# GDN chunk matrices kept in SBUF between preparation and merge, with smaller convolution and inversion buffers

## The chip, the cores and the metric

The kernel runs on one core of a Trainium2 chip. The metric is the device time of one execution in microseconds. Engines are named as in the profile: PE is TensorE, PEld its weight loads, DVE is VectorE, ACT is ScalarE, POOL is GpSimd, SP is SyncE, which here only issues DMAs.

## The reference, cut to what matters

One layer of a diffusion backbone: 256 context tokens and 1024 latent tokens of width 1024; norm and modulation, one input projection, two groups of four heads (a gated DeltaNet, "GDN", and a retention), output projection, SwiGLU, final norm. The change concerns the triangular solve inside the GDN:

```python
A = jnp.where(strict, jnp.einsum('nbhid,nbhjd->nbhij', kb, kc) * decay, 0.0)
rhs = jnp.concatenate([vc * bc[..., None], kb * jnp.exp(G)[..., None]], axis=-1)
sol = lax.linalg.triangular_solve(A + jnp.eye(CHUNK, dtype=A.dtype), rhs,
                                  left_side=True, lower=True, unit_diagonal=True)
...
def step(S, xs):
    u_c, w_c, q_c, qk_c, k_c, gl = xs
    v_new = u_c - jnp.einsum('bhck,bhkv->bhcv', w_c, S)
    o = jnp.einsum('bhck,bhkv->bhcv', q_c, S) + jnp.einsum('bhij,bhjv->bhiv', qk_c, v_new)
    S = gl * S + jnp.einsum('bhck,bhcv->bhkv', k_c, v_new)
    return S, o
```

It runs over the sequence in both directions. q, k and v come from the projection through a centred convolution of five taps and a Silu.

## The kernel before

The kernel works with chunks of 128 tokens: ten chunks (0 and 1 are context), four heads, two directions. For each chunk, head and direction it builds a 128 x 128 triangular matrix, inverts it, and stores the inverse in DRAM (`sd`) for the scan.

Order of the stages that matter. Convolutions: `conv_block` (L596) projects one head of 128 channels for all tokens on PE into the two PSUM banks `b2`, copies each piece twice with ACT (L608 to `u`, L609 to `y`), adds the other four taps on DVE (L615) and applies Silu on ACT (L618). It runs four times for k, four times for q (latent tokens only), four times for v. `y` comes from `newy` (L620), three buffers in the pool CV. A buffer comes free when its heads' transposes have read it: `kstat` (L625) for k, `qstat` (L681) for q, the vT transposes (L868) for v, and when the k or q store (L654, L697) is done. The order of the q loop is written out: the statistics of one head stand behind the convolution of the next and behind `ada_rest` (L487), a modulation product on DVE.

The gate projection rg (`token_major` for groups 6 and 7, L704 and L706) follows q, the z projection (groups 8 and 9, L891) follows the merges, four more projections (groups 2 to 5) follow two scan steps (L999 to L1002). Each projects tiles of 128 tokens with 24 matmuls of 256 columns, stored through `res` (two buffers in R1) to `rd` or `zd`.

The solve goes by three batches of chunks, `BATCH` (L714): sixteen, sixteen and eight matrices per direction.
- `pre(t)` (L719) loads k and q of a chunk, forms the products kk and kq on PE, and for each direction loads the decay row `gw` (L732), masks it on POOL into `e` (L736), takes the exponential on ACT (L740), multiplies kk by it on DVE into `ut` (L744) and kq into `sp` (L746). `ut` is stored to `un` in DRAM (L747), `sp` to `sd` (L749).
- `invert(b)` (L755) loads the diagonal 32 x 32 blocks of all matrices of the batch from `un` into `yr`, one block per partition (L763), copies them to `L`, sets `X` to the identity on POOL (L767, L768) and inverts by 31 pairs of DVE instructions (L777, L779). `X` and its transpose go to `xd` in DRAM (L783).
- `blocks(b)` (L785) loads all of `un` back to SBUF as `U` (L795), clears `t64` (L797), and loads the inverted blocks from `xd` into U and t64 (L799, L800).
- `merge(b)` (L804) builds the inverse of 64 and then of 128 from the blocks with small matmuls (L819 to L846), and stores U to `sd` (L850).

`solve(0)` and `solve(1)` stand ahead of the v convolutions; preparation of batch 2 (chunks 5 and 6) stands behind them and behind the closing of CV; then come `merge(0)`, `invert(2)`, `merge(1)`, `merge(2)`.

SBUF is handed out by pools that open and close from the left (`gu`, `gi`, `gp`, `g2`, weights) and from the right (`gs`, `cv`, `rope`, `gm`, later the scan's). A tile waits for the tiles that lay at its place. The program is written in dependent order, and the framework fixes each engine's order when the kernel is built, by a model of the times; on the chip every engine and every DMA queue runs its own order strictly. The SP queue carries the loads of `pre`, the `un`, `sp`, `xd` transfers and the scan's loads; the ACT queue carries the stores of q, k, v, `res` and merged U, and most weights.

Of the kernel before, what the change touches and what calls it, by code (L numbers as in the profile page):

```python
# [8 lines left out]
F32 = mybir.dt.float32  # L9
# [3 lines left out]
ALU = mybir.AluOpType  # L13
# [4 lines left out]
P = 128  # L18
# [4 lines left out]
NTOK = NCTX + NLAT  # L23
TT = NTOK // P
LT = NLAT // P
H = 4
# [12 lines left out]
def build(nc, tc, ap, dbg=None, stop=None, marks=None):  # L39
# [151 lines left out]
    try:  # L191
# [428 lines left out]
        def newy():  # L620
            return CV.tile([P, NTOK], F32, tag="y", name="y", bufs=3)

# [27 lines left out]
        for h in range(H):  # L650
            y = newy()
# [64 lines left out]

        un = [dr.tile([P, 2, len(ch) * H, P], F32, tag="un%d" % b, name="un%d" % b) for b, ch in enumerate(BATCH)]

        def pre(t):  # L719
            b, c = where[t]  # L720
            kc = load(GP, kd[t], "kc", 2)
            pk = bank_b("kk")
            for h in range(H):
                T.matmul(pk[:, h * P:(h + 1) * P], kc[:, h, :], kc[:, h, :], start=True, stop=True)
            if t >= 2:
                qc = load(GP, qd[t - 2], "qc", 2)
                pq = bank_b("kq")
                for h in range(H):
                    T.matmul(pq[:, h * P:(h + 1) * P], kc[:, h, :], qc[:, h, :], start=True, stop=True)
            for d in range(2):  # L730
                gw = GP.tile([P, H, P], F32, tag="gw", name="gw", bufs=2)
                SY.dma_start(gw.rearrange("p h i -> p (h i)"),  # L732
                             grow_d[c8(t, d), :].rearrange("a b -> (a b)").partition_broadcast(P))
                e = GP.tile([P, H, P], F32, tag="e", name="e", bufs=2)
                sg = 1 if d == 0 else -1
                G.affine_select(out=e, in_=gw, compare_op=ALU.is_ge, fill=FAR, base=0,  # L736
                                pattern=[[0, H], [sg, P]], channel_multiplier=-sg)
                for h in range(H):
                    col = t * 8 + d * 4 + h
                    S.activation(e[:, h, :], e[:, h, :], AF.Exp, bias=sm["nG"][:, col:col + 1])  # L740
                if t >= 2:
                    sp = GP.tile([P, H, P], F32, tag="sp", name="sp", bufs=2)
                ut = GU.tile([P, H, P], F32, tag="ut", name="ut", bufs=2)
                V.tensor_tensor(ut.rearrange("p h i -> p (h i)"), pk, e.rearrange("p h i -> p (h i)"), ALU.mult)  # L744
                if t >= 2:
                    V.tensor_tensor(sp.rearrange("p h i -> p (h i)"), pq, e.rearrange("p h i -> p (h i)"), ALU.mult)  # L746
                SY.dma_start(un[b][:, 1 - d, c * H:(c + 1) * H, :], ut)  # L747
                if t >= 2:
                    SY.dma_start(sd[t, :, 8 - 8 * d], sp.rearrange("p h i -> p (h i)"))  # L749
# [5 lines left out]
        def invert(b):  # L755
# [6 lines left out]
            for k in range(4):  # L762
                SY.dma_start(yr[k:2 * nb:4].rearrange("r (i j) -> r i j", j=32),  # L763
                             un[b][q32[k]].rearrange("i e u j -> (e u) i j")[:, :, q32[k]])
            L = GI.tile([P, 1024], F32, tag="L", name="L", bufs=3)
            X = GI.tile([P, 1024], F32, tag="X", name="X", bufs=2)
            G.memset(X, 0.0)  # L767
# [4 lines left out]
            for j in range(31):  # L772
                n = 31 - j
                tmp = GI.tile([P, 256], F32, tag="tmp%d" % b, name="tmp", bufs=2)
                t3 = tmp[:2 * nb, :n * (j + 1)].rearrange("p (i c) -> p i c", c=j + 1)
                sh = [2 * nb, n, j + 1]
                V.tensor_tensor(t3, bc(m(L)[:, j + 1:, j], sh, 2), bc(m(X)[:, j, :j + 1], sh, 1), ALU.mult)  # L777
                xs = m(X)[:, j + 1:, :j + 1]
                V.tensor_tensor(xs, xs, t3, ALU.subtract)  # L779
            XT = GI.tile([P, 1024], F32, tag="L", name="XT", bufs=3)  # L780
            V.tensor_copy(m(XT), X[:2 * nb].rearrange("p (i j) -> p j i", j=32))
# [3 lines left out]
        def blocks(b):  # L785
# [6 lines left out]

            at = G2 if b == 1 else GM
            uu = at.tile([P, 2, len(BATCH[b]), H, P], F32, tag="U", name="U%d" % b, bufs=1)
            SY.dma_start(uu.rearrange("p e c h j -> p e (c h) j"), un[b])  # L795
            tt = at.tile([P, 2, nu, 64], F32, tag="t64", name="t64", bufs=1)
# [7 lines left out]
        def merge(b):  # L804
# [11 lines left out]
            for n in range(nu):  # L816
                for d, p, a, bb in pairs:
                    ca = (a % 2) * 32
                    T.matmul(ps1[q[bb], n * 32:n * 32 + 32], u[d][q[a], n, q[bb]], t[d][q[a], n, ca:ca + 32],  # L819
                             start=True, stop=True)  # L820
            xt1 = GM.tile([P, 16, 32], F32, tag="xt1", name="xt1", bufs=1)
            V.tensor_scalar(xt1.rearrange("p n j -> p (n j)")[:, :nu * 32], ps1[:, :nu * 32], -1.0, None, ALU.mult)
# [14 lines left out]
            for n0 in range(0, nu, 8):  # L837
                ps1, ps2 = bank_b("m2"), bank_b("m2")
                xt2 = GM.tile([P, 8, 64], F32, tag="xt2", name="xt2", bufs=1)
                for n in range(8):  # L840
# [34 lines left out]
        rope = RP.tile([P, TT, P], F32, tag="rope", name="rope")  # L875
        GM = pool("gm", side="right")
        for t in BATCH[2]:
            pre(t)
# [794 lines left out]
```

## Time and profile before

| What | us |
| --- | --- |
| runs | 1485.98, 1486.84, 1479.36 |
| median of the runs | 1485.98 |
| profiled execution | 1482.3 |
| its span | 1480.4 |
| PE busy | 1399.8 |
| DVE busy | 981.1 |
| ACT busy | 610.5 |
| POOL busy | 579.5 |

The span runs from the first to the last instruction of the profiled execution; the execution's own time also holds what lies around it, 1.9 us. In the span the first k convolution's results are copied at 129 us, the last q convolution's at 262 us; preparation's first multiplication stands at 278.9 us, the last v transposes at 372.6 us, the first merge's matmuls begin at 403.7 us, the last merge's end at 475 us. Lines in the order of time give start, duration, engine, line, operation, output and inputs, the number of merged instructions, and in brackets the idle time before them with what ended it.

### The profile page before, as it was taken

The page shows a single profiled execution, that of the slowest core. Times are in us where ns is not written, and L with a number is a line of the kernel's source. Part 1 is how long each engine was busy: PE and PEld are TensorE (multiplying, and loading weights), DVE is VectorE, ACT ScalarE, POOL GpSimd, SP SyncE. Part 2 cuts the span into 40 slices and gives each one's busy share as a digit, 9 for nine tenths or more (in the row PEclk, how much of TensorE's full clock was granted, in tenths as well). Part 3 has the DMA queues.
Part 4 walks back from the last instruction along what each step waited for, and adds up shares of the span by engine and source line. Part 5 has one row for each costly group of instructions (what it writes and reads, how often), then busy time and mean ns, then how long its engine had stood idle before and what let it go on. Part 6 is the DMA issues. An engine that isn't in the chain of part 4 may idle for free.

```text
span 1480.4 us, 24179 instructions
## 1 busy us (share of the span) xinstructions
PE 1399.8 (95%) x8919; PEld 1200.6 (81%) x8919; DVE 981.1 (66%) x1909; ACT 610.5 (41%) x1336; POOL 579.5 (39%) x493
## 2 busy tenths in 40 slices
PE   7999999997889999998799899999999999999997
PEld 2798888876879999898588688877888888788886
DVE  6568797379772535789677886746555554657586
ACT  5543554765222111446444533323333333454454
POOL 0130010220102353254135588999555553335321
PEclk9999999999899999999799999999999999999999
DMA  9537686696878625985633265765232242786863
GB/s 338 186 104 230 178 245 204 199 297 191 256 193 272 247 69 185 411 328 181 217 115 115 85 215 210 266 240 178 107 107 107 107 150 74 239 279 195 306 202 114
DMA packets 170710, 293.95 MB, mean 199 GB/s; under 512 B 43528, under 2 KB 93912, under 8 KB 166496
## 3 DMA queue, kind: packets, MB, share of 16 engines
q1 hardware_dynamic: 119040, 248.98, 49.3%
q10 hardware_dynamic: 49072, 35.83, 7.7%
q0 software_dynamic: 2480, 7.60, 1.4%
q8 instruction: 70, 1.15, 0.3%
q14 instruction: 48, 0.39, 0.1%
HBM read 206.60 MB, written 85.77 MB: 197 GB/s over the span
## 4 chain that ended last, share of the span: by engine, by line
PE 40%; POOL 6%; DMA 2%; issue 1%; DVE 1%; ACT 0%; POOLq 0%; DVEq 0%; ACTq 0%
PE ffn L1362 7%; PE ffn L1360 6%; PE ffn L1361 6%; PE fo L1486 5%; PE fo L1488 5%; PE fo L1487 5%; DMA wd<-tw 2%; PE op L1219 2%; PE op L1220 2%; PE op L1221 2%; POOL ws L1333 1%; POOL tw L1414 1%; POOL tw L1413 1%; POOL tw L1416 1%; POOL tw L1415 1%
## 5 line engine op out<-in xcount | busy, mean ns | idle before, releaser
L371 PE MATMUL tm<-whi,hhi 128*128 128x256 f32 (+1 forms) x704 | 200.8, 290 | 7.2 <-ACT res L532 3.6
L372 PE MATMUL tm<-wlo,hhi 128*128 128x256 f32 (+1 forms) x704 | 200.4, 287 | 1.3 <-DVE wlo L345 1.3
L373 PE MATMUL tm<-whi,hlo 128*128 128x256 f32 (+1 forms) x704 | 198.7, 287 | 0.0
L371 PEld LDWEIGHTS tm<-whi,hhi 128*128 128x128 f32 x704 | 133.9, 192 | 11.5 <-ACT res L532 4.0
L1360 PE MATMUL ffn<-t,whi 128*128 128x512 f32 x352 | 136.9, 390 | 1.3 <-ACT whi L344 1.3
L1362 PE MATMUL ffn<-t,wlo 128*128 128x512 f32 x352 | 137.0, 390 | 0.8 <-DVE wlo L345 0.8
L372 PEld LDWEIGHTS tm<-wlo,hhi 128*128 128x128 f32 x704 | 134.9, 192 | 3.1 <-DVE wlo L345 1.7
L1361 PE MATMUL ffn<-t,whi 128*128 128x512 f32 x352 | 137.0, 389 | 0.0
L344 ACT ACTIVATE whi<-wraw 128x512 fp32r<-128x512 f32 (+2 forms) x98 | 75.1, 770 | 147.9 <-PE ffn L1361 81.9
L373 PEld LDWEIGHTS tm<-whi,hlo 128*128 128x128 f32 x704 | 134.2, 192 | 0.6 <-DVE hlo L314 0.2
L344 ACT ACTIVATE whi<-ws 128x512 fp32r<-128x512 f32 x88 | 55.6, 632 | 172.5 <-PE ffn L1361 131.3
L345 DVE TENSOR_TENSOR wlo<-ws,whi 128x512 fp32r<-128x512 f32 x88 | 94.0, 1069 | 46.5 <-ACT whi L344 46.3
L1486 PE MATMUL fo<-whi,ahi 128*128 128x512 f32 x308 | 119.3, 389 | 0.7 <-ACT ahi L344 0.7
L1487 PE MATMUL fo<-wlo,ahi 128*128 128x512 f32 x308 | 119.9, 389 | 0.0
L1488 PE MATMUL fo<-whi,alo 128*128 128x512 f32 x308 | 119.0, 390 | 0.0
L345 DVE TENSOR_TENSOR wlo<-wraw,whi 128x512 fp32r<-128x512 f32 (+2 forms) x92 | 100.7, 1097 | 23.4 <-ACT whi L344 23.4
L1360 PE MATMUL ffn<-b,whi 128*128 128x512 f32 x264 | 104.1, 394 | 4.1 <-ACT whi L344 4.1
L1362 PE MATMUL ffn<-b,wlo 128*128 128x512 f32 x264 | 103.9, 393 | 0.7 <-DVE wlo L345 0.7
L1361 PE MATMUL ffn<-b,whi 128*128 128x512 f32 x264 | 103.7, 393 | 0.0
L605 PE MATMUL b<-hhi,whi 128*128 128x512 f32 (+1 forms) x256 | 94.7, 370 | 0.8 <-ACT y L609 0.8
L607 PE MATMUL b<-hhi,wlo 128*128 128x512 f32 (+1 forms) x256 | 94.6, 370 | 0.0
L606 PE MATMUL b<-hlo,whi 128*128 128x512 f32 (+1 forms) x256 | 93.8, 366 | 0.0
(451 smaller groups left out, 3422.0 us busy)
## 6 DMA issues: line engine op xcount, KB each, us to landing
adaw<-ada SPq DMA_DIRECT2D x48, 512.0 KB, 4.6
pk<-sd SPq DMA_DIRECT2D x16, 1536.0 KB, 15.1
wraw<-wfi SPq DMA_DIRECT2D x44, 512.0 KB, 4.5
ar<-ad SPq DMA_DIRECT2D x33, 512.0 KB, 4.4
w<-wfo SPq DMA_DIRECT2D x22, 512.0 KB, 3.6
wd<-tw SPq DMA_DIRECT2D x11, 1024.0 KB, 4.9
ad<-act SPq DMA_DIRECT2D x20, 512.0 KB, 3.2
raw<-wd SPq DMA_DIRECT2D x20, 512.0 KB, 4.8
```

Source lines behind the costliest of these rows:

```text
L344: S.activation(hi, raw, AF.Copy)
L345: e.tensor_tensor(lo, raw, hi.bitcast(F32), ALU.subtract)
L371: T.matmul(o, hhi[:, k, tsl], whi[:, k % 4, :], start=(k == 0), stop=False)
L372: T.matmul(o, hhi[:, k, tsl], wlo[:, k % 4, :], start=False, stop=False)
L373: T.matmul(o, hlo[:, k, tsl], whi[:, k % 4, :], start=False, stop=(k == KT - 1))
L605: T.matmul(o, whi[:, k, :], hh, start=(k == 0), stop=False)
L1360: T.matmul(o, whi[:, k, :], xhi(xn, slice(0, 4), k), start=(first and k == 0), stop=False, **kw)
L1361: T.matmul(o, whi[:, k, :], xlo(xn, slice(0, 4), k), start=False, stop=False, **kw)
L1362: T.matmul(o, wlo[:, k, :], xhi(xn, slice(0, 4), k), start=False, stop=(k == 3), **kw)
L1486: T.matmul(po[g][i], ahi[:, ts], whi, start=(j == 0 and not kw), stop=False, **kw)
L1487: T.matmul(po[g][i], ahi[:, ts], wlo, start=False, stop=False, **kw)
L1488: T.matmul(po[g][i], alo[:, ts], whi, start=False, stop=(j == FH - 1), **kw)
```

## The change

The matrices are multiplied straight into three SBUF tensors U0, U1, U2 of the shape that `merge` uses, and stay there. U0 and U1 lie in GU, on the left, from before `solve(0)`; U2 lies in GM, on the right, opened after the v convolutions. Only the diagonal blocks go to DRAM (`yd`, four strided stores per batch), and from there with one plain load into `yr`. The stores to `un` and the reloads of U go. `e` becomes the same tile as `gw`, which has three buffers in place of two and two. `y` has two buffers in place of three, `L` two in place of three, `X` one in place of two, `tmp` one for all batches in place of two for each; `xt1` and `xt2` share one buffer.

```diff
         def newy():
-            return CV.tile([P, NTOK], F32, tag="y", name="y", bufs=3)
+            return CV.tile([P, NTOK], F32, tag="y", name="y", bufs=2)
...
-        un = [dr.tile([P, 2, len(ch) * H, P], F32, tag="un%d" % b, name="un%d" % b) for b, ch in enumerate(BATCH)]
+        yd = [dr.tile([2 * len(ch) * H, 4, 32, 32], F32, tag="yd%d" % b, name="yd%d" % b) for b, ch in enumerate(BATCH)]
+
+        def matrices(b, pl):
+            return pl.tile([P, 2, len(BATCH[b]), H, P], F32, tag="U%d" % b, name="U%d" % b, bufs=1)
+
+        us = [matrices(b, GU) for b in range(2)]
...
-                gw = GP.tile([P, H, P], F32, tag="gw", name="gw", bufs=2)
+                gw = GP.tile([P, H, P], F32, tag="gw", name="gw", bufs=3)
...
-                e = GP.tile([P, H, P], F32, tag="e", name="e", bufs=2)
+                e = gw
...
-                ut = GU.tile([P, H, P], F32, tag="ut", name="ut", bufs=2)
-                V.tensor_tensor(ut.rearrange("p h i -> p (h i)"), pk, e.rearrange("p h i -> p (h i)"), ALU.mult)
+                V.tensor_tensor(us[b][:, 1 - d, c].rearrange("p h i -> p (h i)"), pk, e.rearrange("p h i -> p (h i)"), ALU.mult)
                 if t >= 2:
                     V.tensor_tensor(sp.rearrange("p h i -> p (h i)"), pq, e.rearrange("p h i -> p (h i)"), ALU.mult)
-                SY.dma_start(un[b][:, 1 - d, c * H:(c + 1) * H, :], ut)
...
             for k in range(4):
-                SY.dma_start(yr[k:2 * nb:4].rearrange("r (i j) -> r i j", j=32),
-                             un[b][q32[k]].rearrange("i e u j -> (e u) i j")[:, :, q32[k]])
-            L = GI.tile([P, 1024], F32, tag="L", name="L", bufs=3)
-            X = GI.tile([P, 1024], F32, tag="X", name="X", bufs=2)
+                SY.dma_start(yd[b][:, k].rearrange("u i j -> i u j"),
+                             us[b][q32[k]].rearrange("p e c h j -> p (e c h) j")[:, :, q32[k]])
+            SY.dma_start(yr[:2 * nb], yd[b].rearrange("u k i j -> (u k) (i j)"))
+            L = GI.tile([P, 1024], F32, tag="L", name="L", bufs=2)
+            X = GI.tile([P, 1024], F32, tag="X", name="X", bufs=1)
...
-                tmp = GI.tile([P, 256], F32, tag="tmp%d" % b, name="tmp", bufs=2)
+                tmp = GI.tile([P, 256], F32, tag="tmp", name="tmp", bufs=1)
...
-            XT = GI.tile([P, 1024], F32, tag="L", name="XT", bufs=3)
+            XT = GI.tile([P, 1024], F32, tag="L", name="XT", bufs=2)
...
             at = G2 if b == 1 else GM
-            uu = at.tile([P, 2, len(BATCH[b]), H, P], F32, tag="U", name="U%d" % b, bufs=1)
-            SY.dma_start(uu.rearrange("p e c h j -> p e (c h) j"), un[b])
+            uu = us[b]
...
-            xt1 = GM.tile([P, 16, 32], F32, tag="xt1", name="xt1", bufs=1)
+            xt1 = GM.tile([P, 16, 32], F32, tag="xt", name="xt1", bufs=1)
...
-                xt2 = GM.tile([P, 8, 64], F32, tag="xt2", name="xt2", bufs=1)
+                xt2 = GM.tile([P, 8, 64], F32, tag="xt", name="xt2", bufs=1)
...
         GM = pool("gm", side="right")
+        us.append(matrices(2, GM))
         for t in BATCH[2]:
             pre(t)
```

## The prediction

> **What bounds the kernel now.** I read the page's busy shares first, then the table of stages, then the waits of TensorE, then the order of time around the longest wait.
>
> ```profile
> PE 1399.8 (95%) x8919; PEld 1200.6 (81%) x8919; DVE 981.1 (66%) x1909; ACT 610.5 (41%) x1336; POOL 579.5 (39%) x493
> ...
> 240.00:360.00 120.00, 112.27 (x743) 99.43 (x742) 82.43 (x137) 74.52 (x210) 21.49 (x24) 1.00 0.72 225
> 360.00:480.00 120.00, 98.20 (x1705) 93.89 (x1705) 74.87 (x184) 35.85 (x66) 15.12 (x23) 0.91 0.80 237
> 480.00:583.00 103.00, 103.00 (x886) 102.98 (x884) 45.36 (x142) 13.46 (x23) 47.69 (x93) 1.00 0.42 149
> ```
>
> TensorE (PE) is busy for 1399.8 of 1480.4 us. In the stage rows the second number is the stage's length, then come PE, its weight loads, VectorE (DVE), ScalarE (ACT), GpSimd (POOL), granted clock, DMA share, GB/s. The change touches work from 128 us (first convolution) to 476 us (last merge). From 480 to 583 PE has no gap at all: the projections there don't depend on the chunk matrices and absorb any shift of the merges. So the change can only be worth what PE idles, or runs at a low clock, before 480: 120 - 112.27 = 7.7 us in the first stage, 120 - 98.20 = 21.8 us in the second.
>
> ```profile
> PE vT L868 <- ACT y L618: 13.1, 3, 11.5
> ...
> 372.64 2.40 PE L868 MATMUL vT<-ident,y 128*128 128x128 f32 x10 [11.54 <-ACT y L618]
> ...
> 393.10 0.39 PE L371 MATMUL tm<-whi,hhi 128*128 128x256 f32 x1 [2.75 <-ACT res L532]
> ...
> 415.45 0.26 PE L829 MATMUL m<-xt,U 32*32 32x32 f32 x2 [3.39 <-issue]
> ```
>
> The 21.8 us have three main places: 11.54 us before the transposes of the last v convolution, 2.75 us at 390 us, and gaps inside the merges (the largest 3.39). The first is a DVE limit, as this part of DVE's order shows:
>
> ```profile
> 359.52 1.22 DVE L345 TENSOR_TENSOR wlo<-wraw,whi 128x1024 fp32r<-128x1024 f32 x1
> ...
> 362.11 1.41 DVE L615 SCALAR_TENSOR_TENSOR y<-u,cw,y 128x1022 f32<-128x1022 f32 x1
> ...
> 365.56 0.68 DVE L744 TENSOR_TENSOR ut<-kk,e 128x512 f32<-128x512 f32 x1
> ...
> 370.01 1.28 DVE L615 SCALAR_TENSOR_TENSOR y<-u,cw,y 128x1022 f32<-128x1022 f32 x1
> ```
>
> PE has finished the convolution by 358 us; the four taps start at 362.11 and end at 371.3, because preparation of chunks 5 and 6 and steps of the first inversion run between them.
>
> The second place is a DMA limit:
>
> ```profile
> ACT res L532 <- DMA zd<-res: 13.2, 3, 8.0
> ...
> 376.98 5.82 SPq L763 DMA_DIRECT2D yr<-un  x4
> 383.18 0.32 SPq L795 DMA_DIRECT2D U<-un  x1
> 392.32 0.34 SPq L883 DMA_DIRECT2D rope<-rope  x1
> ...
> U<-un SPq DMA_DIRECT2D x2, 2048.0 KB, 8.5
> ...
> 390.00:395.00 5.00, 2.25 (x14) 2.05 (x14) 4.62 (x12) 0.73 (x2) 0.00 (x0) 0.86 0.66 177
> 395.00:400.00 5.00, 5.00 (x36) 5.00 (x36) 1.08 (x4) 0.77 (x2) 0.00 (x0) 0.79 1.07 241
> ```
>
> The 2 MB reload of U1 is issued at 383.18 and takes 8.5 us, to 391.7; SP's next issue comes at 392.32. In the same time the gate stores (zd<-res) are late: ACT waits 8.0 us for one, so the two res buffers stay full and PE stands 2.75 us; afterwards the clock is at 0.86 and 0.79.
>
> **The change, part by part.**
>
> *Reloads and un stores.* Twenty un stores of 256 KB and three loads of U (2 + 2 + 1 MB), some 10 MB, go. Added are twelve yd stores of diagonal blocks and three yr loads; the twelve strided yr loads go. SP issues 35 DMAs before and 15 after. At 383 to 392 us this takes the 2 MB of U1 out of a full DMA. I count the 2.75 us stall as gone, and the lost clock with it, (0.14 + 0.21) x 5 = 1.75 us: -4.5 us. Bounds: 0 (the stores are late for another reason) and -4.5.
>
> *The way to the inversion.* Before, the last ut store and four strided loads; after, four strided stores and one plain load. Two hops either way. A 128-byte store to DRAM is not in the trace; the nearest rows are
>
> ```profile
> yr<-un SPq DMA_DIRECT2D x8, 128.0 KB, 5.0
> ...
> U<-xd SPq DMA_DIRECT2D x8, 128.0 KB, 3.5
> ...
> un<-ut SPq DMA_DIRECT2D x20, 256.0 KB, 4.6
> ```
>
> A yd store moves the same 128-byte pieces as a yr load, so I take 5.0 us against 4.6 for the un store it replaces: +0.4 on a chain that PE doesn't wait for directly. Below: nothing, or -1.1 by U<-xd; above: twice 5.0.
> The Trainium skill ("DMA: Bandwidth & Descriptors", Specifications) speaks against this part: below 512 B the DMA engine does a read-modify-write. The trace can't say for stores, as no store before has such pieces; what it would do is a rival below.
>
> *Preparation.* ut with its two buffers goes; DVE writes into U. That ends 8.5 us of DVE waits, and gw with e in place has three buffers where a pair of twos stood:
>
> ```profile
>   DMA un<-ut: 8.5, 3
> ...
> POOL e L736 <- DMA gw<-grow_d: 23.9, 5, 8.5
> ```
>
> These lie between 278 and 337 us, beside the v convolutions, which keep PE at 112 of 120 us. I cost the gain at nothing; it pays for the later start described next. For chunks 5 and 6, U2 now lies where CV was, so their multiplications into U must follow the last v transposes. Two of them (0.68 us each; the second stood at 368.81) ran before the last tap: -1.4 us of the 11.54. Bounds: 0, and -11.5 if the tap order changes altogether. Behind the waiting multiplications only batch 2 is queued.
>
> *Two y buffers.* Three already bind; these rows give the points:
>
> ```profile
> 188.76 0.39 ACT L532 ACTIVATE res<-tm 128x256 f32<-128x256 f32 x1
> ...
> 214.25 0.58 ACT L608 ACTIVATE u<-b 128x512 f32<-128x512 f32 x1
> ...
> 224.75 0.38 PE L632 MATMUL kt<-ident,y 128*128 128x128 f32 x2
> ...
> 225.68 0.69 ACT L609 ACTIVATE y<-b,cw 128x512 f32<-128x512 f32 x1
> ...
> 255.07 0.28 PE L371 MATMUL tm<-whi,hhi 128*128 128x256 f32 x1
> 255.19 0.28 PE L372 MATMUL tm<-wlo,hhi 128*128 128x256 f32 x1
> ...
> 260.73 1.09 PE L686 MATMUL qt<-ident,y 128*128 128x128 f32 x8
> ...
> 262.38 1.26 ACT L609 ACTIVATE y<-b,cw 128x512 f32<-128x512 f32 x2
> ...
> 354.83 0.40 PE L605 MATMUL b<-hhi,whi 128*128 128x512 f32 x1
> ...
> 357.38 0.39 PE L607 MATMUL b<-hhi,wlo 128*128 128x512 f32 x1
> ```
>
> The third q convolution gets its y when k's last transposes end (225.1), the fourth when the first q statistics end (261.8). With two buffers each q convolution moves up one place: the second waits for 225, the third for 262, and the fourth convolves only after 262, since both PSUM banks are held until then. A q convolution is 48 matmuls; the twelve rows from 354.83 to 357.38 are 0.232 us apart, so it takes 11.1 us. PE must be filled otherwise from the end of the second one (its last copy is at 214.25) to 225.7, and from the end of the third (225.7 + 11.1) to 262.4: 11.4 + 25.6 = 37 us. The filler is the rg projection: 16 tiles of 24 matmuls 0.12 us apart, 2.9 us each, 46 us, of which the second tile was stored at 188.76; 40 us are left. It suffices, by 3 us, so I take 0. If it runs out, the fourth convolution is uncovered: +11.1 us is the upper bound, and below nothing, since PE has no gap here to win. The last q store follows this convolution's taps and so comes later, and with it preparation of chunk 2; the un waits that go cover that.
>
> *One X, two L, one tmp.* tmp and L are used in order on DVE and cost nothing. X is different:
>
> ```profile
> 381.43 0.95 POOL L767 MEMSET X<- 128x1024 f32 x1 [7.07 <-DVE X L779]
> ...
> 376.36 0.21 DVE L777 TENSOR_TENSOR tmp<-L,X 128x31 f32<-128x31 f32 x1
> ```
>
> This memset is that of the third inversion: its slot came free only at 381.4, when the first inversion's X stores had landed. With one buffer the second inversion needs this slot, so it starts at 381.43 + 0.95 + 0.16 = 382.5 and not 376.36: 6.2 us later, and the third again. Behind it wait the second merge and the scan's first loads. PE covers this with the z projection and the four projections after it (103 us without a gap above), so I take 0; uncovered it is 6.2, or 12.4 for both. Sharing xt is 0: xt1 has been read when xt2 is written.
>
> **Sum:** 4.5 + 1.4 = 5.9 us off the profiled execution's 1482.3: 1476.4. The median of the runs is 1485.98, 3.7 above it, so I predict **1480.1**; its own range is 1474 to 1486.
>
> **Rivals**, all as the median would show them.
> 1. *The last v stall goes too.* DVE has less to do before the last tap, or the z projection, whose weights are ready by 361 us, is placed ahead of the transposes. Then 11.54 us and the low clock after it (0.50 and 0.84 are granted in the two pieces of 5 us from 370; of PE's 2.35 and 5.00 busy us in them full speed would save 1.2 + 0.8) go with the 4.5: 1485.98 - 18 = 1468. For it: a filler exists. Against: DVE's list there stays nearly full, and an order fixed at build time put the transposes first. Chance 0.20.
> 2. *The single X becomes a wait of PE: slower.* PE runs in a fixed order; if its first matmul of the second merge stands where the inverse used to land, it waits 6.2 us there and 6.2 at the third: +12.4 - 4.5, 1494. It decides from the point at which PE gets there before the xd loads land. For: the merges already show gaps (3.39). Against: 103 us of filler. Chance 0.22.
> 3. *Nothing is gained:* the reloads were hidden and zd is late because of the sd and xd stores: 1486. Chance 0.08.
> 4. *Small stores are slow:* yd stores land in 10 us, and on SP the loads for the first merge stand behind yr of batch 2; 5 us later, that gives back the 4.5: about 1485. Chance 0.05. It is what the Trainium skill's read-modify-write would look like here.
>
> ```profile
> 370.00:375.00 5.00, 2.35 (x11) 2.36 (x12) 4.66 (x13) 2.40 (x4) 1.81 (x1) 0.50 0.95 324
> 375.00:380.00 5.00, 5.00 (x38) 5.00 (x37) 4.45 (x15) 0.79 (x1) 0.00 (x0) 0.84 0.98 357
> ```
>
> **How the numbers follow.** The forecast has 0.45. A measurement of this kernel tells about 0.5%, 7.4 us, from no change: faster means under 1478.6, slower over 1493.4. Half of the forecast's spread lies under 1478.6, with rival 1 that is 0.42 faster; rival 2 makes 0.22 slower; 0.36 is left for no change. The range of 8 in 10 cuts half of rival 1 and half of rival 2: 1467 to 1495.
>
> **What would show it.** Right: no stall of PE on res near 390 us, zd stores landing in under 5 us, a stall before the last vT of 8 to 11 us, the q convolutions' y at about 225 and 262 with PE full, the second inversion's memset right behind the first's stores. Wrong: PE waits on m matmuls for U or t over 3.4 us (rival 2), PE gaps between 215 and 277 (the filler ran out), yd landing above 8 us (rival 4), or a stage from 480 on that changes its length, which none of my steps allows.

## The result and the profile after

The changed kernel takes 1488.67 us (median of 15 runs, 1484.88 to 1492.67), the kernel before, run beside it on the same chip, 1482.71 us (1477.93 to 1486.84). The ratio is 1.0040 with a 95% interval of 1.0026 to 1.0054: the change costs 0.4%, 6 us, where 0.4% of gain was forecast. The profiled execution took 1488.32 us.

First the page's span and busy shares, then the same three stages as in the prediction (length, then PE, PEld, DVE, ACT, POOL, granted clock, DMA share, GB/s), all of the changed kernel.

```profile
span 1486.5 us, 24142 instructions
...
PE 1407.3 (95%) x8919; PEld 1207.9 (81%) x8919; DVE 978.0 (66%) x1909; ACT 618.0 (42%) x1342; POOL 579.6 (39%) x493
...
240.00:360.00 120.00, 112.38 (x690) 97.94 (x689) 76.11 (x119) 75.96 (x203) 21.67 (x22) 0.99 0.66 191
360.00:480.00 120.00, 100.41 (x1497) 95.68 (x1497) 83.41 (x207) 37.56 (x65) 19.62 (x30) 0.89 0.58 153
480.00:583.00 103.00, 101.56 (x1032) 100.64 (x1033) 39.58 (x123) 15.21 (x28) 41.97 (x83) 0.98 0.50 180
```

What the change was to bring is there. Between 360 and 480 us the DMA share fell from 0.80 to 0.58 and PE is busy for 100.41 instead of 98.20 us. But there are 1497 matmuls in that stage where 1705 stood: part of the merges has slipped into the next one, which was without a gap and now lacks 1.4 us of PE and 0.02 of clock. PE's busy time as a whole grew by 7.5 us with the same 8919 matmuls. That is work done at a lower clock. Two windows show it, of the kernel before and then of the changed one:

```profile
300.00:400.00 100.00, 81.03 (x504) 72.38 (x504) 87.21 (x170) 49.37 (x101) 16.77 (x16) 0.93 0.81 252
400.00:500.00 100.00, 93.12 (x1700) 89.39 (x1699) 51.86 (x138) 28.24 (x49) 16.32 (x31) 0.97 0.77 233
```

```profile
300.00:400.00 100.00, 82.18 (x530) 74.42 (x529) 73.59 (x137) 57.57 (x115) 18.55 (x20) 0.93 0.75 208
400.00:500.00 100.00, 89.21 (x1593) 84.21 (x1594) 60.94 (x159) 24.16 (x43) 19.46 (x33) 0.90 0.61 172
```

Idle time of PE in these 200 us went from 18.97 + 6.88 = 25.9 to 17.82 + 10.79 = 28.6 us, while the 3.7 us of idle between 240 and 300 us disappeared. So PE idles no longer than before. The granted clock is either 1 or 0.5 in this trace, so (1 - clock) x 2 x 100 us is the time at half clock: (0.07 + 0.03) x 200 = 20 us before, (0.07 + 0.10) x 200 = 34 us after. In pieces of 5 us, the busy time times (1 - clock) from 100 to 590 us is 6.2 us before and 12.8 after: 6.6 us lost to the clock, 2.5 us won on idle time, 4.1 in all. The last projection matmul before the scan's tail stands at 582.6 instead of 577.8 us, 4.8 later.

Why the clock drops can be read from PE's order of time (start, duration, engine, line, in brackets the idle time before) and from pieces of 5 us in the changed kernel:

```profile
311.86 1.39 PE L734 MATMUL kq<-qc,kc 128*128 128x128 f32 x5 [2.60 <-issue]
...
415.11 0.26 PE L829 MATMUL m<-U,xt 32*32 32x32 f32 x1 [2.57 <-issue]
...
441.85 1.01 PE L371 MATMUL tm<-whi,hhi 128*128 128x256 f32 x3 [3.03 <-ACT whi L344]
...
480.71 0.24 PE L822 MATMUL m<-t,U 32*32 32x32 f32 x2 [2.29 <-DMA t<-xd]
```

```profile
310.00:315.00 5.00, 3.14 (x13) 2.98 (x14) 2.48 (x4) 2.90 (x10) 0.00 (x0) 0.69 0.44 73
...
440.00:445.00 5.00, 2.90 (x12) 2.61 (x13) 3.14 (x5) 2.55 (x4) 0.00 (x0) 0.66 1.01 291
445.00:450.00 5.00, 5.00 (x31) 4.87 (x30) 2.53 (x7) 0.00 (x0) 0.00 (x0) 0.66 1.03 190
```

After a gap of 2.60 us the piece from 310 us has a clock of 0.69; with one of 3.03 us two pieces have 0.66, the second of them with PE busy throughout. Gaps of over 2 us between 290 and 500 us: four before (11.54, 3.39, 2.75, 2.36), six after (8.73, 3.03, 2.64, 2.60, 2.57, 2.29). The long gap is shorter, there are more short ones, and a short one too can bring a stretch at half speed. The Trainium skill ("TensorE: Matmul & The Clock Gate", Part 1) puts the fall to half rate behind a whole idle window of about 3.4 us; the trace here has it with gaps of 2.3 to 3.0 us too, though not with each (2.64 us at 341 us brought none). Finer windows show more: in the changed kernel half clock comes in stretches of 3.41, 6.83 or 10.24 us, and in the 3.41 us before each of the six between 300 and 500 us PE was busy for 0.00 to 2.05 us. The gap of 2.64 us fell into two such steps, with 2.00 and 2.18 us busy, and no half clock followed; one of 1.32 us at 399 us fell into one, with 2.05 us busy, and it did. In the traces of all twenty kernels here, from 100 us on, half clock followed each of the 156 full-speed steps of 3.41 us in which PE was busy for less than 1.4 us and none of the 7406 in which it was busy for more than 2.41 us; of the 210 between, 33. What counts is thus how a gap falls into these steps, and not its length alone.

What is late ahead of these gaps: preparation starts 11.4 us later. First the kernel before, then the changed one: the last Silu of a q head, its transposes, and the first product of preparation.

```profile
273.41 1.05 ACT L618 ACTIVATE y<-y 128x1024 f32<-128x1024 f32 x1
...
276.59 1.03 PE L686 MATMUL qt<-ident,y 128*128 128x128 f32 x8
277.59 0.97 PEld L724 LDWEIGHTS kk<-kc 128*128 128x128 f32 x8
```

```profile
284.72 1.06 ACT L618 ACTIVATE y<-y 128x1024 f32<-128x1024 f32 x1 [2.34 <-DVE y L615]
...
288.25 1.03 PE L686 MATMUL qt<-ident,y 128*128 128x128 f32 x8
...
289.12 1.06 PE L729 MATMUL kk<-kc 128*128 128x128 f32 x8
```

The q statistics and kk share PSUM banks, so kk of chunk 0 follows the last head's statistics directly. And the merges end late, as the rows grouped by tile show (count, min/median/max ns, first to last start), before and after: the inversions' products, and the merges' last kind of matmuls.

```profile
L777 DVE TENSOR_TENSOR tmp<-L,X x93: 182/359/584, 313.7 to 441.6; 128x31 f32<-128x31 f32 x4, 128x60 f32<-128x60 f32 x4, 128x87 f32<-128x87 f32 x4, 128x112 f32<-128x112 f32 x4
...
L846 PE MATMUL m<-U,xt x160: 218/218/267, 427.7 to 474.5; 64*64 64x64 f32 x160
```

```profile
L781 DVE TENSOR_TENSOR tmp<-L,X x93: 183/357/677, 332.8 to 469.0; 128x31 f32<-128x31 f32 x4, 128x60 f32<-128x60 f32 x4, 128x87 f32<-128x87 f32 x4, 128x112 f32<-128x112 f32 x4
...
L849 PE MATMUL m<-U,xt x160: 217/218/267, 427.7 to 498.6; 64*64 64x64 f32 x160
```

11 us at preparation's start became 19 at the first inversion, 27 at the last and 24 at the last merge. That these delays make the gaps isn't shown by the two traces alone.

### The profile page after: what moved, and what is told of

Read it like the earlier page. It is cut to its first block, busy times and chain, and to the rows that moved or that the text cites. A ratio compares the mean times of both kernels' runs of the same rounds, so it can differ in the third digit from the quotient of the medians.

```text
span 1486.5 us, 24142 instructions
## 1 busy us (share of the span) xinstructions
PE 1407.3 (95%) x8919; PEld 1207.9 (81%) x8919; DVE 978.0 (66%) x1909; ACT 618.0 (42%) x1342; POOL 579.6 (39%) x493
## 5 line engine op out<-in xcount | busy, mean ns | idle before, releaser
L615 DVE SCALAR_TENSOR_TENSOR y<-u,cw,y 128x1022 f32<-128x1022 f32 (+3 forms) x80 | 81.9, 1040 | 19.7 <-ACT y L609 19.2
```

## The experiments

Each kernel was timed in five rounds beside the kernel before. Ratios are to it, with 95% intervals. Single profiled executions differ from the medians by several us either way, so sizes come from the ratios. After the two traces three explanations stood open: two y start preparation late; one X holds the merges up; the tile of gw and e in place slows preparation down.

**One part at a time, on the kernel before.**

```diff
-            return CV.tile([P, NTOK], F32, tag="y", name="y", bufs=3)
+            return CV.tile([P, NTOK], F32, tag="y", name="y", bufs=2)
```

> The kernel before with one edit: two y buffers in place of three. Theory Y (the y buffers make preparation late): the fourth q convolution can start only after the first q statistics at about 260 us, its statistics come at about 288 us instead of 276.6, the first kk matmul at about 289 instead of 277.7, and the ratio to before is 1.003 to 1.006. Theory X (the single X buffer makes the later inversions and merges late): first kk late too, but the time within 1.000 to 1.002, since PE has the v convolutions then. Theory G (gw and e in one tile): 1.000 to 1.002.

Measured: 0.9965 (0.9952 to 0.9979). Its first kk stands at 287.2 us, almost as late as in the changed kernel, and its merges end at 476.5:

```profile
287.19 1.06 PE L724 MATMUL kk<-kc 128*128 128x128 f32 x8
...
L846 PE MATMUL m<-U,xt x160: 218/218/267, 424.5 to 476.5; 64*64 64x64 f32 x160
```

A late start of preparation by itself costs nothing. None of the three theories had a gain; where its 0.35% comes from was not found.

```diff
-            L = GI.tile([P, 1024], F32, tag="L", name="L", bufs=3)
-            X = GI.tile([P, 1024], F32, tag="X", name="X", bufs=2)
+            L = GI.tile([P, 1024], F32, tag="L", name="L", bufs=2)
+            X = GI.tile([P, 1024], F32, tag="X", name="X", bufs=1)
...
-                tmp = GI.tile([P, 256], F32, tag="tmp%d" % b, name="tmp", bufs=2)
+                tmp = GI.tile([P, 256], F32, tag="tmp", name="tmp", bufs=1)
```

> The kernel before with only the inversion's buffers cut: one X, two L, one tmp. Theory X: the memset of the second inversion waits for the first one's xd stores (near 382 us), the last merge ends 10 us or more later than 475 us, ratio 1.003 to 1.006. Theory Y: the inversions move the same way but PE covers it, 0.999 to 1.002. Theory G: 0.999 to 1.002.

Measured: 1.0003 (0.9990 to 1.0015). The merges end 11.9 us later and the time is the same: the projections cover the single X, as the prediction had it.

```profile
L846 PE MATMUL m<-U,xt x160: 218/218/267, 421.4 to 486.4; 64*64 64x64 f32 x160
```

```diff
-                gw = GP.tile([P, H, P], F32, tag="gw", name="gw", bufs=2)
+                gw = GP.tile([P, H, P], F32, tag="gw", name="gw", bufs=3)
...
-                e = GP.tile([P, H, P], F32, tag="e", name="e", bufs=2)
+                e = gw
```

> The kernel before with only gw and e made one tile with three buffers. Theory G: POOL's wait for gw loads grows from 23.9 towards the 61.4 us of the changed kernel, preparation runs slower, ratio 1.003 to 1.006. Theories Y and X: the wait may grow, but it is beside the v convolutions: 0.998 to 1.002.

Measured: 1.0112 (1.0089 to 1.0134), 16 us. This small edit alone costs more than the whole change, and about twice the most that theory G gave it. ScalarE's order of time in this kernel shows one reason:

```profile
272.77 1.28 ACT L740 ACT_TABLE_LOAD   x1
274.06 0.69 ACT L740 ACTIVATE gw<-gw,nG 128x128 f32<-128x128 f32 x2
274.77 1.28 ACT L618 ACT_TABLE_LOAD   x1
276.07 1.06 ACT L618 ACTIVATE y<-y 128x1024 f32<-128x1024 f32 x1
277.03 0.26 ACT L688 ACTIVATE qt<-qt 128x128 f32<-128x128 f32 x1
...
277.43 1.28 ACT L740 ACT_TABLE_LOAD   x1
278.73 0.40 ACT L740 ACTIVATE gw<-gw,nG 128x128 f32<-128x128 f32 x1
...
279.32 0.25 ACT L688 ACTIVATE qt<-qt 128x128 f32<-128x128 f32 x1
...
280.00 1.28 ACT L532 ACT_TABLE_LOAD   x1
...
282.57 1.97 PE L686 MATMUL qt<-ident,y 128*128 128x128 f32 x8 [5.40 <-ACT qt L688]
```

With three loads ahead, exponentials of the first chunks (L740) are placed before the last Silu (L618) and among the squares of the q statistics (L688), each time with a change of table (12 loads of 1.28 us from 255 to 480 us, 8 in the kernel before). The squares are late, and PE stands 5.40 us for the PSUM bank that they hold. The Trainium skill ("ScalarE: Activation LUTs", What ACT_TABLE_LOAD costs) counts some 1.4 us of drain on top of each load; here the load's 1.28 us is all that can be seen, since the exponential at 278.73 starts 0.02 us after the load that began at 277.43 ends.

**The changed kernel with three y for k and q, two for v** (CV is closed after q and opened again):

```diff
-        def newy():
-            return CV.tile([P, NTOK], F32, tag="y", name="y", bufs=2)
+        def newy(bufs=3):
+            return CV.tile([P, NTOK], F32, tag="y", name="y", bufs=bufs)
...
+        close(CV)
+        CV = pool("cv2", side="right")
...
-            y = newy()
+            y = newy(2)
```

> The changed kernel with three y buffers for the k and q convolutions (the pool is closed after q and opened again with two for v). Theory Y: first kk at about 278 us again, first inversion's first step near 318 us instead of 332.8, last merge's end near 480 instead of 498, ratio to before 0.997 to 1.000. Theory X and theory G: first kk moves back, but the ratio stays at 1.003 to 1.005.

Measured: 0.9978 (0.9963 to 0.9994). That is 0.6% under the changed kernel: the third y, without which the kernel before was even 0.35% faster, decides the sign here.

```profile
277.90 1.05 PE L731 MATMUL kk<-kc 128*128 128x128 f32 x8
...
L851 PE MATMUL m<-U,xt x160: 218/218/267, 406.9 to 476.7; 64*64 64x64 f32 x160
```

The first kk, the merges' end and the ratio are all where theory Y put them. The run also closes and reopens the pool of the convolutions; that by itself, with two y throughout, was not run.

**Is the tile in place too shallow?** Four buffers on the kernel before, and gw and e apart in the changed one, where the 10 KB of gw and sp allow two of one and three of the other with the second product written into e:

```diff
-                gw = GP.tile([P, H, P], F32, tag="gw", name="gw", bufs=2)
+                gw = GP.tile([P, H, P], F32, tag="gw", name="gw", bufs=4)
...
-                e = GP.tile([P, H, P], F32, tag="e", name="e", bufs=2)
+                e = gw
```

> The kernel before with gw and e as one tile in place, as in the run that changed this alone and cost 1.1%, but with four buffers, which takes the same 8 KB as two of gw and two of e. Left out: nothing. Theory N (three buffers are too few: a load of 5 us can be issued only when the vector multiplications of three halves earlier are through): GpSimd's wait for gw falls from 83 us to at most 35, preparation keeps its pace, ratio 0.997 to 1.003. Theory S (in place itself costs, because the four exponentials and the select share one tile and what waits for it, however many there are): the wait stays above 60 us and the ratio is 1.007 to 1.012.

Measured: 1.0072 (1.0055 to 1.0088). That is in the range of S, though the fourth buffer took 0.4% away and GpSimd's wait for gw fell to 54 us, between the two theories. The table loads rose to 14: with four buffers still more exponentials run ahead.

```diff
-                gw = GP.tile([P, H, P], F32, tag="gw", name="gw", bufs=3)
+                gw = GP.tile([P, H, P], F32, tag="gw", name="gw", bufs=2)
...
-                e = gw
+                e = GP.tile([P, H, P], F32, tag="e", name="e", bufs=3)
...
-                    sp = GP.tile([P, H, P], F32, tag="sp", name="sp", bufs=2)
+                    sp = e
```

> The changed kernel with gw and e apart again: two buffers of gw, three of e, and the product with the query matrix written into e instead of a tile sp of its own, which takes the same 10 KB as three of gw and two of sp. The rest of the change stays (matrices in SBUF, two y, one X, two L, one tmp). Theory G (the tile in place is what made the change slower): GpSimd's wait for gw falls from 61 us to 35 or less and the ratio to the kernel before is 0.992 to 0.997, which is 0.4% less than 1.004 at the least. Rival R (the residency itself, or late preparation with all buffers small, costs): the wait falls but the ratio stays 1.001 or more. A third: e held until the store of the product has landed (3 to 5 us) makes the select wait for that instead, then the select's wait on the store of sd shows 20 us or more and the ratio is 0.998 to 1.004.

> As the run before it, but three buffers of gw and two of e: loads go one half further ahead, the select waits longer for e. If the load's way is what sets the pace, the wait for gw goes below that of two and three, and the time is the same or up to 0.2% less; if the release of e sets it (by the store of the product), GpSimd waits on that store above 20 us and the time is 0.2 to 0.6% more.

> The changed kernel with two of gw and three of e (product in e) and with three y buffers for k and q, two for v. With three y alone the changed kernel came to 0.998. Theory G with additive parts: both repairs together give 0.989 to 0.995, below either alone. Rival: both repair the same loss (preparation late and slow), then it is within 0.2% of the better of the two.

Measured: 1.0018 (1.0002 to 1.0034), 1.0039 (1.0023 to 1.0055) and, with three y, 0.9992 (0.9977 to 1.0007). Theory G's ranges are missed: with gw and e apart the changed kernel gains 0.2% at most, and beside three y nothing. The third case named in the first expectation is what the trace shows; GpSimd now waits for the store of the product (30.6 us in 8 waits, 40.7 with three of gw and two of e, which is 0.2% slower, as its expectation had it). So these runs put one wait in another's place and don't show by themselves what the tile in place costs in the changed kernel.

**The residency alone.** The kernel before with all the small buffers of the changed one (two y, the inversion's, gw/e in place, xt shared), un, ut and the reloads kept:

> The kernel before with every buffer as in the changed one (two y, one X, two L, one tmp, shared xt, gw and e one tile of three) but with un stores, ut and reloads of U kept: the whole change except that the matrices stay in SBUF. Theory A (parts add up: two y 0.9965, inversion 1.0003, gw 1.0112): ratio 1.005 to 1.010, so that the residency itself is worth 0.1 to 0.6%. Rival (the parts don't add; late preparation hides the tile in place): at most 1.003, and the residency itself costs something.

Measured: 1.0177 (1.0152 to 1.0201). Its windows:

```profile
300.00:400.00 100.00, 70.03 (x395) 62.38 (x394) 68.09 (x125) 52.24 (x111) 19.37 (x18) 0.84 0.80 255
400.00:500.00 100.00, 90.37 (x1426) 85.92 (x1426) 61.47 (x161) 22.41 (x40) 14.05 (x27) 0.90 0.57 153
```

Both theories missed it. The product of the three parts is 0.9965 x 1.0003 x 1.0112 = 1.0080; together they cost more than twice that. Its merges end at 524.2 us, and its half-clock time is (0.16 + 0.10) x 200 = 52 us. Between this kernel and the changed one lies only the residency, with its own way to the inversion: 1.0040 / 1.0177 = 0.9865, some 20 us of gain. Taken in this order, the change consists of small buffers that cost 1.8% and of a residency that gains 1.3% beside them. What it would gain beside larger buffers was not measured.

**Run-ahead.** The exponentials read their bias from a copy of nG to which zero times the last q statistic is added, so none can stand ahead of the squares:

```diff
+        nGq = GP.tile([P, TT * 8], F32, tag="nGq", name="nGq", bufs=1)
+        V.scalar_tensor_tensor(nGq, nq[:, LT - 1, H - 1:H].to_broadcast([P, TT * 8]), 0.0, sm["nG"],
+                               ALU.mult, ALU.add)
...
-                    S.activation(e[:, h, :], e[:, h, :], AF.Exp, bias=sm["nG"][:, col:col + 1])
+                    S.activation(e[:, h, :], e[:, h, :], AF.Exp, bias=nGq[:, col:col + 1])
```

On the kernel before with gw/e in place (three buffers):

> The kernel before with gw and e one tile of three buffers (1.0112 alone), and the exponentials read their bias from a copy of nG to which zero times the last q statistic is added: one small VectorE instruction more, and no exponential can stand ahead of the last squares of the q statistics in ScalarE's order. Theory O (with the tile in place three halves of exponentials run ahead on ScalarE, in front of the squares that free the PSUM bank of the first kk): TensorE's 5.4 us wait for the squares near 280 us goes, the first kk moves from 284.8 to 280 us or earlier, ratio 1.000 to 1.006. Theory L (the load's turnaround alone: the next load waits for VectorE's products): GpSimd's wait for gw stays above 70 us and the ratio at 1.008 or more.

Measured: 1.0069 (1.0050 to 1.0088), between the two; GpSimd's wait for gw is 44.9 us, under the 70 of theory L. The wait of 5.4 us is gone from the waits of PE (240 to 300 us, total, times, longest), the first kk stands at 275.6:

```profile
PE kq L732 <- issue: 1.0, 1, 1.0
PE tm L372 <- DVE wlo L345: 0.8, 1, 0.8
PE kk L727 <- DMA kc<-sd: 0.2, 1, 0.2
```

With its own gw and e (the control), and with four buffers in place:

> The kernel before with its own gw and e (two buffers each) and only the bias that makes the exponentials follow the last q statistic: the control for the runs that have this bias. Both theories: TensorE has no wait for the squares to lose here, so 0.998 to 1.003; what it differs from 1 is to be taken off the run that has the bias and the tile in place (1.0069).

> The kernel before with gw and e one tile of four buffers, and the exponentials held behind the last q statistic. With three buffers and this bias it was 1.0069, with four and no bias 1.0072, with three and no bias 1.0112. Theory D (two causes: run-ahead on ScalarE, which four buffers make worse, and too little depth, which they mend): both mended, ratio 0.998 to 1.003, GpSimd's wait for gw 40 us or less. Theory S (in place itself costs whatever the depth): 1.005 to 1.010.

Measured: 1.0017 (1.0006 to 1.0029) and 0.9996 (0.9981 to 1.0011). With run-ahead stopped and a fourth buffer, the tile in place costs nothing. Either repair alone leaves 0.7% (0.5% for the hold, where the control's 0.17% is taken off): two causes, depth and run-ahead, as theory D has it. One sign that it named is wrong. GpSimd waits even longer for gw, and the kernel is fast:

```profile
POOL gw L739 <- DMA gw<-grow_d: 72.9, 18, 24.1
```

So that wait, by which I had found the tile in the first place, is no measure of its cost: it is time of an engine that has little to do.

On the changed kernel:

> The changed kernel with the same bias, so that its exponentials too begin only after the last q statistic (289 us; they began at 266). Theory O: ScalarE's table loads between 255 and 480 us fall from 14 to 10 or less, ratio to before 0.998 to 1.002, 0.2 to 0.6% under that of the changed kernel. Theory L: late start of the exponentials costs what it takes away, 1.003 to 1.008.

Measured: 1.0042 (1.0026 to 1.0059). That is in theory L's range. The table loads fell from 14 to 10 as theory O expected, and nothing is won by it: PE is full from 240 to 300 us in the changed kernel and has no wait for the squares to lose.

> The changed kernel with three y for k and q, and gw and e apart again, two buffers each, paid for by one sp buffer in place of two. With three in e and the product written there the select waited 53 us for the stores and the ratio was 0.9992; with gw in place and three y it was 0.9978. Theory G with the tile apart as before: 0.992 to 0.996. Rival: the single sp, freed by the store of 256 KB, holds VectorE's products instead, VectorE's wait on the store of sp passes 20 us and the ratio is 0.998 or more.

Measured: 1.0013 (0.9999 to 1.0028): two of gw and e each, paid for by the second sp, is 0.35% slower than the tile in place. The ratio is in the rival's range, but VectorE's wait on the store of sp is 15.9 us, under the 20 that the rival named; what costs here stays open.

**How much is the built order alone?** The load of q written ahead of the four kk products instead of behind them, first in the kernel before, then in the changed one:

```diff
+            if t >= 2:
+                qc = load(GP, qd[t - 2], "qc", 2)
             pk = bank_b("kk")
...
             if t >= 2:
-                qc = load(GP, qd[t - 2], "qc", 2)
                 pq = bank_b("kq")
```

> The kernel before with two lines of preparation swapped that don't depend on each other: the load of q is written ahead of the four kk products in place of behind them. Same work, same buffers, same waits; but the order that the framework fixes for each engine comes out different from preparation on. Theory N (such a difference of order alone is worth little): 0.998 to 1.002. Rival (the built order moves the time as much as the parts of the change do): off by 0.4% or more in either direction, and then differences of that size between the runs can't be given to a buffer.

> The changed kernel (1.004) with the same two lines swapped. Theory N: 1.002 to 1.006. Rival: outside of it, by 0.4% or more from 1.004 in either direction.

Measured: 0.9999 (0.9982 to 1.0016) and 1.0056 (1.0042 to 1.0070). Both lie in theory N's ranges, but they don't test it: in the traces of both pairs ScalarE, VectorE, GpSimd and the DMA queues run the same instructions on the same tiles in the same order, and TensorE's 8919 matmuls differ only in a few dozen places, among small merge matmuls that run side by side. The swap, against the expectation, didn't change the built order. So the 0.0 and 0.16% tell how far two measurements of one order lie apart, and differences of 0.2% aren't to be given to a buffer. What another order alone is worth stays unmeasured. The other edits do change it (two y in the kernel before: 741 of VectorE's 1909 places), so a part of any of these ratios may be order.

**The repairs together.** gw, e and sp as one tile of five buffers (the same 10 KB), exponentials held; then with three y for k and q as well:

```diff
-                gw = GP.tile([P, H, P], F32, tag="gw", name="gw", bufs=3)
+                gw = GP.tile([P, H, P], F32, tag="gw", name="gw", bufs=5)
...
-                    sp = GP.tile([P, H, P], F32, tag="sp", name="sp", bufs=2)
+                    sp = gw
```

> The changed kernel with gw, e and sp as one tile of five buffers in place (10 KB as before: three of gw, two of sp), and the exponentials held behind the last q statistic. On the kernel before, four buffers and that hold took the loss by the tile in place from 1.0112 to 0.9996. Theory D carried over: 0.996 to 1.001, at least 0.3% under the changed kernel's 1.004. Rival (here the two y buffers set the pace, since the q statistics end 11 us later anyway): 1.002 to 1.006.

> The same with three y buffers for k and q and two for v. With three y alone the changed kernel came to 0.998. Theory D: 0.991 to 0.996, the best of all. Rival (both mend the same late and slow preparation): 0.996 to 1.000.

Measured: 1.0029 (1.0015 to 1.0042) and 0.9956 (0.9938 to 0.9973), 1476.35 us: the fastest median of the kernels run here, under both the kernel before and the changed one, in the range of theory D (its interval overlaps with the rival's range and with that of the kernel before with two y, 0.9965). Against the 0.9978 of three y alone it is 0.2%, no more than measurements of one order differ by. Without the third y the rival's range holds, that of two y buffers that set the pace. The step from two to three y is worth 0.73% here, 0.62% without the other repair. Windows of this last kernel:

```profile
300.00:400.00 100.00, 81.25 (x778) 71.57 (x777) 80.59 (x159) 45.93 (x94) 15.65 (x16) 0.91 0.68 195
400.00:500.00 100.00, 97.31 (x1423) 93.13 (x1424) 56.25 (x150) 27.39 (x48) 20.80 (x39) 0.97 0.66 205
```

From 400 to 500 us PE is busy for 97.31 us, against 93.12 before and 89.21 in the changed kernel. How much of that is the residency isn't shown: no kernel with these buffers and without it was run.

| Kernel | ratio | half-clock time, 300 to 500 us |
| --- | --- | --- |
| before | 1 | 20 |
| before, two y | 0.9965 | 20 |
| before, inversion's buffers | 1.0003 | 20 |
| before, gw/e in place | 1.0112 | 32 |
| before, all small buffers | 1.0177 | 52 |
| changed | 1.0040 | 34 |
| changed, three y for k and q | 0.9978 | 24 |
| the same, one tile of five, held | 0.9956 | 24 |

The last column is worked out from the two windows of 100 us of each kernel, one execution each. It is highest where the ratio is, but it doesn't give the ratio: the kernel before with gw/e in place and the exponentials held, which isn't in the table, has 40 us at 1.0069, and the changed kernel 34 at 1.0040. That the clock would recover if the gaps alone were closed was not tried.

## Why the prediction was wrong

The time lies in the range (1467 to 1495), and the case in which nothing moves by more than 0.5% had 0.36. The forecast of 1480.1 has the wrong sign: the interval of the ratio excludes 1. That the range holds the time is luck: its upper part was there for rival 2, with waits of 6.2 us at the second and at the third merge, and the longest wait of that kind is 2.29 us. The chances have a slip too: of the forecast's own range, 1474 to 1486, 4.6 of 12 us lie under 1478.6, not half, which makes faster 0.37 and not 0.42.

*Reloads (-4.5): right in kind.* PE's wait on res near 390 us is gone, zd stores land in 3.1 us (4.5 before), the clock from 380 to 400 us is 1.00. The lost clock was taken over the whole 5 us of each piece; over PE's busy time it is 0.14 x 2.25 + 0.21 x 5 = 1.4 us and not 1.75. As a size it was too small where buffers are scarce: the two kernels that differ only in the residency are 20 us apart. The bound of -4.5 came from one stall of a kernel with larger buffers.

*yd stores and yr loads (+0.4 beside the path): no cost came, and the size was too high.* DMA issues of the changed kernel (count, KB each, median us to landing):

```profile
zd<-res ACTq DMA_DIRECT2D x16, 128.0 KB, 3.1
...
yd<-U SPq DMA_DIRECT2D x8, 128.0 KB, 2.6
yr<-yd SPq DMA_DIRECT2D x2, 512.0 KB, 4.1
yd<-U SPq DMA_DIRECT2D x4, 64.0 KB, 3.7
```

Stores in pieces of 128 bytes land in 2.6 and 3.7 us, where 5.0 was taken. The rival of slow small stores, 10 us, is out. The read-modify-write below 512 B that the Trainium skill states ("DMA: Bandwidth & Descriptors", Specifications) can't be seen in these landings.

*The last v stall (-1.4): right in kind,* 8.73 instead of 11.54 us, -2.8. In one execution more than that came back elsewhere:

```profile
371.08 0.48 PE L871 MATMUL vT<-ident,y 128*128 128x128 f32 x1 [8.73 <-ACT y L618]
```

*gw with e in place ("I cost the gain at nothing; it pays for the later start"): wrong.* Three in place of two and two is a loss, 1.12% alone. The prediction counted buffers. It didn't ask until when each is held (the load's tile now until VectorE's products) nor what an earlier load lets run ahead on ScalarE. In the changed kernel the repairs bring only 0.1 to 0.2%, no more than measurements of one order differ by.

*Two y buffers (0): the step that failed.* Put at nothing, this term measured 0.62 to 0.73%, some 9 to 11 us, beside the other small buffers. The filler was counted correctly: q's y stand at 223.14 and 260.09 us, and PE is full from 240 to 300 us.

```profile
223.14 1.27 ACT L609 ACTIVATE y<-b,cw 128x512 f32<-128x512 f32 x2
...
260.09 1.26 ACT L609 ACTIVATE y<-b,cw 128x512 f32<-128x512 f32 x2
```

But the sentence "the last q store follows this convolution's taps and so comes later, and with it preparation of chunk 2; the un waits that go cover that" saw only the store. The q statistics of the last head move too, they hold the PSUM banks of kk, and all preparation starts 11.4 us later, chunk 0 included. The un waits did go, but the delay grew on its way to the merges, from 11 to 24 us. In the changed kernel a third y for k and q takes 0.62% off, with the tile of five 0.73%, each more than the whole loss of 0.40%. In the kernel before nearly the same late start cost nothing, so it is not the delay alone but the delay together with something else of the change; which part, the runs leave open.

*One X (0): right alone, not in company.* With only the inversion's buffers the time is the same. In the changed kernel the second rival's wait exists in small: PE waits on t<-xd for 4.8 us in four places, 2.29 at the longest, where it was priced at 12.4. "103 us of filler" holds but for 1.4 us of idle time in that stage; it doesn't hold for the clock, which gaps of 2 to 3 us came with at half. The last projection matmul came 4.8 us later, and a change in the stage from 480 us on is what the prediction had named as allowed by none of its steps. Two y together with one X, and nothing else, was not run, nor was the changed kernel with two X. That this pair is what stretches the merges from 474.5 to 498.6 us is argued from the traces and not shown; that all small buffers together cost 1.77% and not the 0.80% of their product is shown.

## What to carry to other kernels

A change that pays for residency by shrinking buffers is two changes: run the small buffers without the residency, and what the residency is worth beside them is known (here 1.8% paid, 1.3% gained back). Before merging two tiles into one, note from which load to which last read each buffer is held, and what the in-order engine in the middle will run ahead with. When delays are said to be covered, follow the moved work to every bank and tile it shares, not just to the transfer that is visibly late. And before an edit counts as a control for the built order, look in the trace whether the order is another.

## What the runs showed that was not expected

Short gaps can cost twice: around 2.57 us of idle time before 415 us and 3.03 us before 442 us TensorE ran at half clock for 6.83 us each, so that in these two executions six scattered gaps of 2 to 9 us cost more than four with a longer one among them, although the idle time summed from 100 to 590 us fell from 31.2 to 28.7 us. And a wait of 73 us of GpSimd for its loads went with a ratio of 0.9996, one of 24 us in the kernel before with 1: the engine that waits longest was not the one to mend.
